# Normalisation transposes in a PSUM bank of their own behind the state update, and the GLU second in the tail

## The chip, the cores and the metric

The kernel runs on one core of a Trainium2 chip. The metric is the time on the device of one execution, in microseconds (us), the median of several runs. The engines are named as in the profile: PE is TensorE (matmuls; PEld its weight loads), DVE is VectorE, ACT is ScalarE, POOL is GpSimd, SP is SyncE, which here only issues DMAs.

## The reference

One layer of a streaming encoder: a prompt of 1024 rows and 8 samples of 16 rows, together T = 1152 rows of width 1024. One input projection feeds four mixers: "a" (S5 state space with GELU and a GLU), "b" (sparse attention), "c" (gated delta rule) and "d" (gated linear attention, GLA). Then

```
x <- LayerNorm(alpha * x + W_out( sum_b sigmoid(r_b(x)) * P_b( silu(z_b(x)) * M_b(x) ) ))
```

For the change, the end of one block of "c" and "d" matters. With state s (per head, 128x128 in "c", 64x128 in "d"):

```
# c, per block
v_new = u_blk - w_blk s
o = exp(gc) * (q s) + ((q k^T) * decay) v_new
s = exp(g_last) * s + (k * exp(g_last - gc))^T v_new
# d, per block
o = A v + (q * exp(bc)) s
s = exp(b_last) * s + (k * exp(b_last - bc))^T v
# both, after all blocks
o = o * rsqrt(mean(o*o) + 1e-6) * norm          # then gated with silu(z)
```

and for "a", `g = y @ w_glu; y = g[:512] * sigmoid(g[512:])`.

## The kernel before

Everything is fp32; large products are made of three fp32r matmuls (`mm3`, L189 to L191: high by high, low by high, high by low), with the operands split into a high part by ACT and a low part by DVE or POOL.

Tiles of 128 rows: nine of them, 0 to 7 the prompt, 8 the samples. The program is written stage after stage, and a planner that simulates the engines lays down, ahead of time, the order of instructions on every engine. It prefers what has the higher priority among what it believes ready: DMA loads and splits marked urgent first, then the mixers and the tail in the order of the program, then, as filler, the products of the input projection (`gemm_t`, tile pg). On the chip each engine works its list in order, and a semaphore wait holds up all behind it.

PSUM has eight banks: two for pg, two for pn, four for pm. `pmt` hands out the four pm banks in turn, in the order of the program; nearly all products and transposes of sparse attention, delta rule and linear attention go through them, and so do the final products (L1834 region, tile fin).

Delta rule, `gdn_tile(i)`, for each tile i: loads; small products that finish a triangular inverse (m1, u1, x1); then products kq, pv, kn, ks (L978), qs (L983), each evacuated by DVE (L960, L965, L970, L980, L984); vn (L1009), copied to VN by ACT; oi (L1014), from which DVE makes o (L1020). Then `rms_gate`: ACT squares o, DVE makes rsqrt of the mean in small steps (L652 to L657), scales o (L1063), PE transposes it into the pm tile py (L1066), DVE multiplies with norm and gate (L1068) and SP stores to `YD["c"]`. After it the state update: S products (L1025) from kdec and VN, and DVE adds them to the state (L1030). Tile 8 updates eight sample states, four heads one after another, loading and storing them (L1041 to L1051). Most tiles of this stage have one buffer. The state K.S of tile i is read by ks and qs of tile i+1.

Linear attention has the same shape: `gla_levels` for two tiles (seven levels, products lv, L1209), then `gla_scan` for each: glo (L1278), `rms_gate` into `YD["d"]`, then the state products glS (L1289) and updates (L1295). Tile 8 comes first here. `s5` ("a") runs beside delta rule; it uses pn and DVE.

The tail. `mix_branch` reads a branch's output from `YD` in three chunks of 384 rows, splits it, and for 8 column tiles x 3 chunks makes 12 matmuls each into a PSUM tile (mix); DVE multiplies with the merge gate (L1785) and adds to ACC (L1786, from the second branch on). `s5_glu` reads S5's output (12 loads), makes 8 x 3 tiles (glu); the even column tiles go through Tanh on ACT (L1731), the odd ones through DVE twice (L1735, L1737) and are stored to `YD["a"]` (L1738), which `mix_branch` of "a" loads again (L1756). There are four Y buffers: the three chunks of the present step and the first of the next. The order is "b", "c", GLU, "a", "d", then `finish` with W_out and LayerNorm. Tail products that are ready fill PE while linear attention still runs.

Of the kernel before, what the change touches and what calls it, by code (L numbers as in the profile page):

```python
# [67 lines left out]
def setup(K):  # L68
    nc, tc, ctx = K.nc, K.tc, K.ctx
    K.prio, K.kind = {"hi": 0, "lo": 20000000}, None  # L70
    tc.cur_priority = 10000000
    K.const = ctx.enter_context(tc.tile_pool(name="const", bufs=1))
    K.dram = ctx.enter_context(tc.tile_pool(name="dram", bufs=1, space=DRAM))
    K.pg = ctx.enter_context(tc.tile_pool(name="pg", bufs=2, space=PSUM))
    K.pm = ctx.enter_context(tc.tile_pool(name="pm", bufs=4, space=PSUM))
    K.pn = ctx.enter_context(tc.tile_pool(name="pn", bufs=2, space=PSUM))
    c = K.const
    ii = c.tile([128, 128], I32, name="ii")
    K.ident = c.tile([128, 128], F32, name="ident")
    with urgent(K):  # L80
        nc.gpsimd.iota(ii, pattern=[[1, 128]], base=0, channel_multiplier=-1)
        nc.vector.tensor_scalar(K.ident, ii, 0.0, None, op0=OP.is_equal)
    K.colmrow = ii
    K.bd = c.tile([128, 128], F32, name="bd")
    with tc.tile_pool(name="bdp", bufs=1) as t:
        r16 = t.tile([128, 128], I32, name="r16")
        nc.gpsimd.iota(r16, pattern=[[16, 8], [0, 16]], base=0, channel_multiplier=-1)
        hi = t.tile([128, 128], F32, name="hi16")
        nc.vector.tensor_scalar(hi, r16, 0.0, None, op0=OP.is_le)
        lo = t.tile([128, 128], F32, name="lo16")  # L90
        nc.vector.tensor_scalar(lo, r16, -15.0, None, op0=OP.is_ge)
        nc.vector.tensor_tensor(K.bd, hi, lo, op=OP.mult)
    K.bdneg = c.tile([128, 128], F32, name="bdneg")
    nc.vector.tensor_scalar(K.bdneg, K.bd, BIG, -BIG, op0=OP.mult, op1=OP.add)
# [797 lines left out]
def gdn_tile(K, i, tp):  # L892
# [125 lines left out]
    else:  # L1018
        for h in range(4):
            nc.vector.scalar_tensor_tensor(o[:, h], po[:, H4[h]], rq[:, h:h + 1], tmp[:, h], op0=OP.mult, op1=OP.add)  # L1020
    rms_gate(K, o, K.gnorm, gt, tp, "c", s)
    if i < 8:
        pS = pmt(K, "S")
        for h in range(4):
            nc.tensor.matmul(pS[:, H4[h]], kdec[:, h], VN[:, h], start=True, stop=True)  # L1025
        if i == 0:
            nc.vector.tensor_copy(K.S, v4(pS))
        else:
            for h in range(4):
                nc.vector.scalar_tensor_tensor(K.S[:, h], K.S[:, h], eg[:, h:h + 1], pS[:, H4[h]], op0=OP.mult, op1=OP.add)  # L1030
        if i == 7:
            nc.sync.dma_start(O["p_gdn"].rearrange("h k v -> k h v"), K.S)
    else:
        ge = tp.tile([128, 4, 8], F32, tag="ge", name="ge")
        gb = tp.tile([128, 4, 8], F32, tag="gb", name="gb")
        nc.vector.tensor_tensor(gb, K.g[:, 8, :, None].to_broadcast([128, 4, 8]), K.bm[:, None, :].to_broadcast([128, 4, 8]), op=OP.mult)
        pg = pmt(K, "ge")
        nc.tensor.matmul(pg[:, 0:32], K.ones, gb.rearrange("p h b -> p (h b)"), start=True, stop=True)
        nc.scalar.activation(ge.rearrange("p h b -> p (h b)"), pg[:, 0:32], AF.Exp)
        for h in range(4):  # L1040
            S8 = tp.tile([128, 8, 128], F32, tag="S8", name="S8")  # L1041
            nc.sync.dma_start(S8, s8(I["state_gdn"], h))
            for q in range(2):
                vm = tp.tile([128, 4, 128], F32, tag="vt", name="vm")
                nc.vector.tensor_tensor(vm, VN[:, h, None, :].to_broadcast([128, 4, 128]), bc(K.bm[:, q * 4:q * 4 + 4]), op=OP.mult)
                pS = pmt(K, "S8")
                nc.tensor.matmul(pS, kdec[:, h], vm.rearrange("p b v -> p (b v)"), start=True, stop=True)
                for b in range(4):
                    bb = q * 4 + b
                    nc.vector.scalar_tensor_tensor(S8[:, bb], S8[:, bb], ge[:, h, bb:bb + 1], pS[:, H4[b]], op0=OP.mult, op1=OP.add)  # L1050
            nc.sync.dma_start(s8(O["s_gdn"], h), S8)  # L1051


def rms_gate(K, o, norm, gt, tp, br, s):

    nc = K.nc
    ss = tp.tile([128, 4], F32, tag="oss", name="oss")
    junk = tp.tile([128, 128], F32, tag="ojunk", name="ojunk")
    for h in range(4):
        nc.scalar.activation(junk, o[:, h], AF.Square, accum_out=ss[:, h:h + 1])  # L1060
    nc.vector.tensor_scalar(ss, ss, 1.0 / 128.0, 1e-6, op0=OP.mult, op1=OP.add)
    rsqrt(K, ss, ss, tp, 4)
    nc.vector.tensor_tensor(o, o, bc(ss), op=OP.mult)  # L1063
    py = pmt(K, "py")
    for h in range(4):
        nc.tensor.transpose(py[:, h * 128:(h + 1) * 128], o[:, h], K.ident)  # L1066
    yt = tp.tile([128, 4, 128], F32, tag="oyt", name="oyt")
    nc.vector.scalar_tensor_tensor(yt, py.rearrange("p (h t) -> p h t", h=4), norm, gt, op0=OP.mult, op1=OP.mult)  # L1068
    nc.sync.dma_start(K.YD[br].rearrange("(j p) t -> p j t", p=128)[:, :, s], yt)
# [148 lines left out]
def gla_scan(K, i, AT, tp):  # L1218
# [63 lines left out]
        nc.vector.tensor_copy(o, pov)  # L1282
    else:
        nc.vector.tensor_tensor(o, pov, oi, op=OP.add)
    rms_gate(K, o, K.dnorm, gt, tp, "d", s)
    if i < 8:
        for j in range(2):
            pS = pmt(K, "glS")
# [11 lines left out]
    else:  # L1300
# [19 lines left out]
        for z in range(2):  # L1320
            for h in range(4):
                nc.gpsimd.dma_start(O["s_gla"][z::2, h].rearrange("b k v -> k b v"), S8[z * 64:z * 64 + 64, h])


def gla(K):
# [463 lines left out]
def tail(K):  # L1789
    tc = K.tc  # L1790
    with tc.tile_pool(name="mx", bufs=2) as p, tc.tile_pool(name="ap", bufs=1) as ap, \
            tc.tile_pool(name="yb", bufs=3) as yp:
        K.ACC = ap.tile([128, 8, T], F32R, name="ACC")
        K.wo = K.ctx.enter_context(tc.tile_pool(name="wo", bufs=1, side="right"))
        mix_branch(K, 0, "b", yp, p)
        mix_branch(K, 1, "c", yp, p)
        s5_glu(K, 2, yp, p)
        mix_branch(K, 3, "a", yp, p)
        mix_branch(K, 4, "d", yp, p, last=True)
        finish(K, yp, p)  # L1800
# [159 lines left out]
def build(ctx, tc, I, O, stages, dev=None):  # L1960
# [15 lines left out]
    with tc.tile_pool(name="xp", bufs=1) as K.xp, ExitStack() as wn, ExitStack() as nat:  # L1976
# [3 lines left out]
        with tc.tile_pool(name="cvc", bufs=1) as K.cvc:  # L1980
            gdn_prepare(K)
            K.glmask = gla_masks(K)
            with tc.tile_pool(name="bp", bufs=1) as K.bp:
                with ExitStack() as cv:
                    natural_cols(K)
                    nat.close()
                    project_q(K)

                    def between():
                        project_rest(K, "end" in stages)  # L1990
                        wn.close()
                        K.cvp = cv.enter_context(tc.tile_pool(name="cvp", bufs=2, side="right"))
                        project(K, "end" in stages)
                    dsa(K, between)
            if "c" in stages:
                gdn(K)
            gdn_conv_state(K)
# [38 lines left out]
```

## Time and profile before

| | us |
|---|---|
| median of 3 runs | 1908.05 (1903.02 to 1910.44) |
| the profiled execution | 1909.76 |
| its span, first to last instruction | 1908.0 |
| PE busy | 1804.6 |
| DVE busy | 1447.6 |
| ACT busy | 670.9 |
| POOL busy | 270.9 |

The mean granted clock of PE was 0.982 of full speed. The clock has two levels, 1.2 and 2.4 GHz, which the views show as 0.50 and 1.00; a stretch between them had both. In a timeline, the number in brackets is how long the engine sat idle before the instruction, and what released it. A matmul's duration overlaps with that of the next, so counts in a stretch say more than durations.

### The profile page before, as it was taken

To read this page: it belongs to the slowest core of one execution; us is meant where nothing else is said; L and a number is where in the kernel's file an instruction comes from. 1 tells how busy PE (TensorE), PEld (TensorE's weight loads), DVE (VectorE), ACT (ScalarE), POOL (GpSimd) and SP (SyncE) were. 2 spreads that over 40 slices of the span, in tenths; PEclk is the share of its full clock that TensorE was granted. 3 is DMA by queue.
4 is the path that set the end of the run, shared out by engine and by line. 5 is a ranking of instruction groups with operands and counts; after the bars stand their busy time and mean duration, and the time that the engine had idled before them with its cause. 6 is when DMAs were issued, how large, how long until landed. Compare 5 with 4: busy or idle time off the path is not lost.

```text
span 1908.0 us, 31158 instructions
## 1 busy us (share of the span) xinstructions
PE 1804.6 (95%) x10962; PEld 1710.1 (90%) x10962; DVE 1447.6 (76%) x3914; ACT 670.9 (35%) x1535; POOL 270.9 (14%) x297
## 2 busy tenths in 40 slices
PE   8999999999999999998989989899898999979997
PEld 7989999999989999997889888888888998979986
DVE  6289999944999997368890279976657899857776
ACT  4261211233666656245321333332373233222200
POOL 1110222111222210101211112211232000000000
PEclk9999999999999999999999899999999999989999
DMA  6322322232323212467335545444455673376422
GB/s 192 99 67 74 89 90 84 90 101 86 96 75 84 69 55 67 115 214 232 102 96 136 160 134 144 139 134 128 123 166 166 188 173 104 109 229 188 143 88 89
DMA packets 345290, 234.54 MB, mean 123 GB/s; under 512 B 82891, under 2 KB 327419, under 8 KB 345134
## 3 DMA queue, kind: packets, MB, share of 16 engines
q1 hardware_dynamic: 337262, 220.88, 40.1%
q10 hardware_dynamic: 7488, 10.62, 1.5%
q8 instruction: 87, 1.43, 0.3%
q0 software_dynamic: 384, 1.05, 0.2%
q14 instruction: 69, 0.57, 0.1%
HBM read 156.12 MB, written 76.35 MB: 122 GB/s over the span
## 4 chain that ended last, share of the span: by engine, by line
PE 39%; DVE 13%; DMA 5%; issue 3%; ACT 2%; POOL 1%; SPq 1%; DVEq 0%; POOLq 0%; ACTq 0%
PE pg L190 4%; PE pg L191 4%; PE pg L189 4%; PE mix L189 3%; PE mix L190 3%; PE mix L191 3%; PE fin L191 2%; PE fin L190 2%; PE fin L189 2%; PE lv L1209 1%; PE glu L191 1%; PE glu L190 1%; PE glu L189 1%; DMA S<-in_state_gdn 1%; DVE pb L870 1%
## 5 line engine op out<-in xcount | busy, mean ns | idle before, releaser
L189 PE MATMUL pg<-XH,whi 128*128 128x384 f32 x1648 | 564.0, 342 | 0.9 <-DVE gth L238 0.9
L190 PE MATMUL pg<-XL,whi 128*128 128x384 f32 x1648 | 564.3, 342 | 0.0
L191 PE MATMUL pg<-XH,wlo 128*128 128x384 f32 x1648 | 563.4, 342 | 0.0
L189 PEld LDWEIGHTS pg<-XH,whi 128*128 128x128 f32 x1648 | 312.7, 190 | 5.2 <-issue 1.8
L191 PEld LDWEIGHTS pg<-XH,wlo 128*128 128x128 f32 x1648 | 312.5, 190 | 4.1 <-issue 2.0
L190 PEld LDWEIGHTS pg<-XL,whi 128*128 128x128 f32 x1648 | 312.6, 190 | 3.1 <-issue 1.1
L109 ACT CAST whi<-wst 128x1024 fp32r<-128x1024 f32 (+2 forms) x121 | 109.5, 907 | 253.6 <-PE pg L190 118.1
L110 POOL TENSOR_TENSOR wlo<-wst,whi 128x1024 fp32r<-128x1024 f32 x44 | 109.6, 2492 | 335.3 <-ACT whi L109 329.6
L189 PE MATMUL mix<-YH,whi 128*128 128x384 f32 x384 | 132.7, 347 | 13.1 <-ACT YH L112 9.4
L110 DVE TENSOR_TENSOR wlo<-wst,whi 128x512 fp32r<-128x512 f32 (+2 forms) x77 | 76.4, 993 | 77.5 <-ACT whi L109 76.6
L190 PE MATMUL mix<-YL,whi 128*128 128x384 f32 x384 | 131.9, 344 | 1.1 <-DVE YL L113 1.1
L191 PE MATMUL mix<-YH,wlo 128*128 128x384 f32 x384 | 131.9, 344 | 0.0
L1684 ACT ACTIVATE mth<-pg 128x384 f32<-128x384 f32 x96 | 46.7, 487 | 138.3 <-PE pg L191 95.6
L392 DVE TENSOR_SCALAR_CACHE_REDUCE tkj<-mk,tk_c 128x384 bf16<-128x384 f32 (+6 forms) x112 | 90.9, 875 | 0.6
L392 DVE TENSOR_SCALAR_CACHE_REDUCE tkj<-tkh,tk_c 128x384 bf16<-128x384 bf16 (+6 forms) x112 | 90.9, 876 | 0.5
L189 PEld LDWEIGHTS mix<-YH,whi 128*128 128x128 f32 x384 | 73.4, 192 | 15.2 <-ACT YH L112 10.0
L190 PEld LDWEIGHTS mix<-YL,whi 128*128 128x128 f32 x384 | 73.3, 191 | 1.6 <-DVE YL L113 1.5
L191 PEld LDWEIGHTS mix<-YH,wlo 128*128 128x128 f32 x384 | 73.3, 191 | 0.0
L715 DVE SCALAR_TENSOR_TENSOR cy<-rb,cw,cy 128x384 f32<-128x384 f32 (+1 forms) x108 | 71.2, 659 | 2.8 <-ACT cy L713 2.2
L535 ACT ACTIVATE pr<-pr,sm 128x256 f32<-128x256 f32 (+7 forms) x72 | 53.7, 747 | 13.7 <-DVE sm L534 13.5
L1785 DVE SCALAR_TENSOR_TENSOR mth<-mth,mix 128x384 f32<-128x384 f32 x72 | 39.0, 549 | 24.1 <-PE mix L191 12.0
L502 POOL TENSOR_TENSOR mb<-BT,mk 128x512 f32<-128x512 f32 (+1 forms) x32 | 42.8, 1340 | 97.9 <-DVE mx L529 94.7
(630 smaller groups left out, 3794.9 us busy)
## 6 DMA issues: line engine op xcount, KB each, us to landing
wst<-in_w_in SPq DMA_DIRECT2D x80, 512.0 KB
wst<-in_w_branch SPq DMA_DIRECT2D x32, 256.0 KB
gk<-cq SPq DMA_DIRECT2D x27, 256.0 KB
merge_b<-mth SPq DMA_DIRECT2D x24, 192.0 KB
cq<-cy SPq DMA_DIRECT2D x24, 192.0 KB
merge_c<-mth SPq DMA_DIRECT2D x24, 192.0 KB
kq<-cq SPq DMA_DIRECT2D x18, 256.0 KB
merge_d<-mth SPq DMA_DIRECT2D x24, 192.0 KB
```

The source lines that it names most:

```text
L109: nc.scalar.copy(hi, src)
L110: (eng or nc.vector).tensor_tensor(lo, src, hi.bitcast(F32), op=OP.subtract)
L189: nc.tensor.matmul(ps, lh, rh, start=start, stop=False)
L190: nc.tensor.matmul(ps, lh, rl, start=False, stop=False)
L191: return nc.tensor.matmul(ps, ll, rh, start=False, stop=stop)
L392: nc.vector.tensor_scalar(junk[a % 2][:, :ns[a]], up[a] if bit > 15 else sc[a], cand[:, a:a + 1].bitcast(F32), None, op0=OP.is_ge, op1=OP.add,
L502: bias = nc.gpsimd.tensor_tensor(mbv, bt[:, 2 * jj:2 * jj + 2, ::-1][:, :, 256 - band:], mk[:, None, off:n].to_broadcast([128, 2, band]), ...
L535: nc.scalar.activation(p[:, r, 0:n], p[:, r, 0:n], AF.Exp, bias=sm[:, 2 + r:3 + r], scale=1.0, accum_out=sm[:, r:r + 1])
L715: nc.vector.scalar_tensor_tensor(yc, rb[:, i:i + c], K.cw[:, i * 12 + a:i * 12 + a + 1], yc, op0=OP.mult, op1=OP.add)
L870: nc.vector.tensor_tensor(pb[:, lo:bs, 0:lo], ab[:, j, lo:bs, None].to_broadcast([n, bs - lo, lo]), xb[:, j, None, 0:lo].to_broadcast([n, ...
L1684: nc.scalar.activation(th[:, :n], ps, AF.Tanh, scale=0.5)
L1785: nc.vector.scalar_tensor_tensor(th, th, 1.0, ps, op0=OP.add, op1=OP.mult)
```

## The change

The pool pm is made last of the three PSUM pools and closed after sparse attention; a pool of three banks takes its place (same tag, handed out by `pmt`), and the freed bank becomes a pool pr, for py alone. In `gdn_tile` and `gla_scan` the call of `rms_gate` moves behind the state update. In the tail, `s5_glu` changes places with branch "c"; the first argument only says which Y buffers are used.

```diff
@@ setup
     K.pg = ctx.enter_context(tc.tile_pool(name="pg", bufs=2, space=PSUM))
-    K.pm = ctx.enter_context(tc.tile_pool(name="pm", bufs=4, space=PSUM))
     K.pn = ctx.enter_context(tc.tile_pool(name="pn", bufs=2, space=PSUM))
+    K.pm4 = ExitStack()
+    K.pm = K.pm4.enter_context(tc.tile_pool(name="pm", bufs=4, space=PSUM))
@@ gdn_tile
-    rms_gate(K, o, K.gnorm, gt, tp, "c", s)
     if i < 8:
         pS = pmt(K, "S")
...
             nc.sync.dma_start(s8(O["s_gdn"], h), S8)
+    rms_gate(K, o, K.gnorm, gt, tp, "c", s)
@@ rms_gate
-    py = pmt(K, "py")
+    py = K.pr.tile([128, 512], F32, tag="py", name="py")
@@ gla_scan
-    rms_gate(K, o, K.dnorm, gt, tp, "d", s)
     if i < 8:
         for j in range(2):
             pS = pmt(K, "glS")
...
                 nc.gpsimd.dma_start(O["s_gla"][z::2, h].rearrange("b k v -> k b v"), S8[z * 64:z * 64 + 64, h])
+    rms_gate(K, o, K.dnorm, gt, tp, "d", s)
@@ tail
         mix_branch(K, 0, "b", yp, p)
-        mix_branch(K, 1, "c", yp, p)
-        s5_glu(K, 2, yp, p)
+        s5_glu(K, 1, yp, p)
+        mix_branch(K, 2, "c", yp, p)
         mix_branch(K, 3, "a", yp, p)
         mix_branch(K, 4, "d", yp, p, last=True)
@@ build
                     dsa(K, between)
+            K.pm4.close()
+            K.pm = ctx.enter_context(tc.tile_pool(name="pm3", bufs=3, space=PSUM))
+            K.pr = ctx.enter_context(tc.tile_pool(name="pr", bufs=1, space=PSUM))
             if "c" in stages:
                 gdn(K)
```

## Rows read from the trace of the kernel before

**Rows 1.** The page, busy time of each engine, share of the span, instructions.

```profile
PE 1804.6 (95%) x10962; PEld 1710.1 (90%) x10962; DVE 1447.6 (76%) x3914; ACT 670.9 (35%) x1535; POOL 270.9 (14%) x297
```

**Rows 2.** Busy time by stage: PE, PEld, DVE, ACT, POOL; PE clock, DMA share, GB/s.

```profile
1050.00:1280.00 230.00, 207.19 (x1491) 189.76 (x1489) 176.20 (x509) 79.66 (x236) 49.12 (x41) 0.96 0.49 141
1280.00:1420.00 140.00, 130.97 (x765) 121.30 (x765) 85.20 (x196) 57.89 (x99) 31.06 (x35) 0.98 0.47 137
1420.00:1655.00 235.00, 221.98 (x1375) 213.66 (x1374) 206.06 (x487) 75.25 (x178) 17.16 (x17) 0.99 0.54 150
1685.00:1701.00 16.00, 6.35 (x21) 5.95 (x22) 6.53 (x7) 3.39 (x3) 0.00 (x0) 0.68 0.68 217
1701.00:1800.00 99.00, 98.26 (x557) 97.56 (x556) 72.69 (x118) 24.68 (x28) 0.00 (x0) 1.00 0.65 204
```

**Rows 3.** What PE waited for: us in total, times, longest.

```profile
PE mix L189 <- ACT YH L112: 9.4, 2, 8.6
PE py L1066 <- DVE o L1063: 8.7, 5, 4.2
...
PE cs L734 <- DVE S L1050: 4.8, 2, 3.1
...
PE mix L189 <- DVE mth L1785: 3.2, 3, 2.2
...
PE qs L983 <- DVE P L960: 2.2, 2, 1.1
```

**Rows 4.** Timeline, the end of the GLU and the start of branch "a".

```profile
1684.30 0.32 SPq L1738 DMA_DIRECT2D y_a<-glgt  x1
...
1687.52 1.33 SPq L1756 DMA_DIRECT2D yl<-y_a  x2
...
1692.01 1.48 ACT L112 ACTIVATE YH<-yl 128x1536 fp32r<-128x1536 f32 x1 [6.58 <-DMA yl<-y_a]
...
1693.54 0.69 PE L189 MATMUL mix<-YH,whi 128*128 128x384 f32 x1 [8.64 <-ACT YH L112]
...
1696.66 0.32 SPq L1738 DMA_DIRECT2D y_a<-glgt  x1
```

**Rows 5.** Busy time in three stretches of 2 us, columns as in rows 2.

```profile
1230.00:1232.00 2.00, 1.49 (x11) 1.23 (x11) 2.00 (x5) 0.00 (x0) 0.00 (x0) 1.00 0.26 73
1274.00:1276.00 2.00, 2.00 (x10) 2.00 (x11) 1.97 (x4) 0.00 (x0) 0.99 (x1) 0.50 0.06 18
1698.00:1700.00 2.00, 2.00 (x8) 2.00 (x8) 1.00 (x3) 0.00 (x0) 0.00 (x0) 0.50 0.54 118
```

**Rows 6.** Instructions grouped by line, DVE in the tail.

```profile
L1786 DVE TENSOR_TENSOR ACC<-ACC,mth 128x384 f32<-128x384 f32 x72 | 39.2, 553 | 0.8
L1785 DVE SCALAR_TENSOR_TENSOR mth<-mth,mix 128x384 f32<-128x384 f32 x72 | 39.0, 549 | 24.1 <-PE mix L191 12.0 <-DMA mth<-merge_d 5.1 <-DMA mth<-merge_a 2.9
...
L1737 DVE SCALAR_TENSOR_TENSOR glgt<-glth,glgt 128x384 f32<-128x384 f32 x12 | 10.2, 856 | 0.8 <-DMA glgt<-gate_a 0.5
...
L1735 DVE SCALAR_TENSOR_TENSOR glth<-glth,glu 128x384 f32<-128x384 f32 x12 | 6.5, 551 | 4.1 <-PE glu L191 4.1
```

**Rows 7.** Timeline of PE, the end of delta-rule tile 7.

```profile
1258.77 1.05 PE L1014 MATMUL oi<-VN,P 128*128 128x128 f32 x8
...
1273.92 1.11 PE L1066 MATMUL py<-ident,o 128*128 128x128 f32 x4 [4.16 <-DVE o L1063]
1274.83 1.91 PE L1025 MATMUL S<-VN,kdec 128*128 128x128 f32 x8
```

**Rows 8.** All S products: count, duration, first and last start.

```profile
L1025 PE MATMUL S<-VN,kdec x64: 275/275/418, 1081.8 to 1276.3; 128*128 128x128 f32 x64
```

**Rows 9.** Timeline of DVE, the same tile.

```profile
1260.38 1.12 DVE L1020 SCALAR_TENSOR_TENSOR o<-oi,rq,tmp 128x128 f32<-128x128 f32 x4
...
1273.19 0.67 DVE L1063 TENSOR_TENSOR o<-o,oss 128x512 f32<-128x512 f32 x1
```

**Rows 10.** Timeline of PE, delta-rule tile 6.

```profile
1230.51 1.16 PE L983 MATMUL qs<-S,kq 128*128 128x128 f32 x8 [1.12 <-DVE P L960]
```

## The prediction

> **What bounds the kernel now.** I read the page's busy table first, then busy time by stage, then what TensorE (PE) waited for, and last the timeline at two places. PE is busy 1804.6 us of 1908.0 [rows 1]. No later engine can hide that: the work of PE is the same after the change, so the time can fall only where PE stands idle or runs at its lower clock. The stages [rows 2] say where that is. From 1050 to 1420 us (delta rule, with S5 beside it and w_in products as filler) PE is idle 230 - 207.2 + 140 - 131.0 = 31.8 us. From 1420 to 1655 us (linear attention, with filler and the first tail products) it is idle 235 - 222.0 = 13.0 us. From 1685 to 1701 us it does 21 matmuls in 16 us, at a mean clock of 0.68. After that it is full: 557 matmuls in 99 us, 98.26 us busy, which is 0.176 us a matmul.
>
> So a chain that gets shorter on VectorE (DVE) or ScalarE (ACT) is worth nothing in itself. It counts only by the PE stalls that go with it. The list of PE's waits [rows 3] names those: 9.4 us before a mix product for YH, 8.7 us in five waits of the normalisation transposes py, 4.8 us at the conv-state transposes, 3.2 us of mix products for a PSUM bank that L1785 frees, 2.2 us at L983 for a bank that L960 frees. Because the engine works its queue in order, each is a hole in everything, filler too.
>
> **GLU second.** The 9.4 us is the step from the GLU to branch "a". The timeline there [rows 4] shows the chain: a GLU store to y_a is issued at 1684.30, the reload yl<-y_a at 1687.52, ACT starts the split at 1692.01, PE starts at 1693.54 after 8.64 us idle. The twelfth GLU store is issued only at 1696.66, so the third chunk comes later still. PE then runs at granted clock 0.50, the 1.2 GHz level, from 1698 to 1700 [rows 5], after having stood still; 8 matmuls take those 2 us, against 11.4 at 0.176 us. The whole price of the step: 16 us in which 21 x 0.176 = 3.7 us of work was done [rows 2], so 12.3 us. With the change branch "c" (8 x 3 x 12 = 288 matmuls, about 51 us at 0.176) lies between the GLU's last store and branch "a", and the chain of some 10 us is hidden by it five times over. What is late next: at the new steps GLU to "c" and "c" to "a" the operand is ready in DRAM long before, as it is now at "a" to "d", and that step lies inside the stretch 1701 to 1800 where PE lost 0.7 us in all. If the cover were gone, the 12.3 us would be back. I take a gain of 12, with bounds 10 and 13.
>
> The GLU's own loads move too: twelve y loads, the weight and gate loads and twelve stores on SP's queue, 50 to 75 us earlier, past the loads of "c" and among those of linear attention. What can be hurt is linear attention's own loads, where one stands behind them in the queue. I take 0, with a bound of 2.2 us on the bad side (the 2.2 us hole of L983 as the nearest row for a short queue upset).
>
> On DVE a branch tile costs 0.549 + 0.553 us (L1785, L1786), a GLU tile half as often 0.551 + 0.856 us (L1735, L1737), so 0.70 us on the mean [rows 6]. In the stretch where linear attention keeps DVE busy 206 of 235 us [rows 2], 24 GLU tiles stand in place of 24 tiles of "c": 24 x 0.4 = 9.6 us less DVE work there. PE waits 3.2 us for L1785 in the whole run [rows 3]. I take 1 of these, bounds 0 and 3.2.
>
> **State update ahead of the normalisation.** No instruction is added or taken away: nine tiles each of delta rule and linear attention, four transposes, the same DVE and ACT operations, the same store. What changes is the order and the bank. The S products need only VN and kdec. Yet in delta-rule tile 7 they start at 1274.83, 16.1 us after the oi products at 1258.77 and directly behind py at 1273.92 [rows 7]: py sits ahead of S in one ring of four banks and must wait for the chain on DVE, L1020 at 1260.38 to L1063 at 1273.19 [rows 9], lengthened by S5 operations queued between. The eight S groups lie from 1081.8 to 1276.3 [rows 8], so a tile takes about (1274.8 - 1081.8) / 7 = 27.6 us, of which S waits 16 in tile 7. After the change S can follow oi at once and the next tile's first products need no longer stand behind py. My estimate is that a tile falls to between 14 and 20 us and that delta rule ends 60 to 100 us earlier. That moves no end by itself: the filler now used there is used later, PE's work is the same.
>
> What counts is py's holes: 8.7 us [rows 3], and after the longest (4.16 us) PE ran at 0.50 from 1274 to 1276 [rows 5, 7]. That is 2 us at half rate, 1 us lost, so py's price is some 9.7 us. The transposes still wait for the same DVE chain, and they still stand in PE's queue at a place fixed ahead of time. Only the work that was stuck behind them (S, the next tile's products) now has a chance to come before. I take 4 of 9.7, bounds 0 and 9.7. The normalisation now starts behind the four S updates on DVE, and in the last tile behind the whole update of the sample states; the only reader of its store is a tail branch, so this is 0. The next tile's gate load (L908) waits on SP for L1068, now later, and weight loads stand behind it: two weight buffers of 72 matmuls each (12.7 us at 0.176) cover a few us, 0 again. The conv-state transposes (4.8 us) wait for the last state updates, which the change brings ahead of the normalisation but does not shorten: 0.
>
> By the Trainium skill, "TensorE: Matmul & The Clock Gate", section "HAM oscillation", PSUM double-buffering on top of a loop already kept dense gave no further gain (126.6 against 125.5 us). By that rule a private bank would be worth 0 and the sum would end 4 us later; the row of py differs in kind, as the bank here holds back other work, and no run here shows it yet.
>
> **Three banks for the rest.** From delta rule on, every other pm tile turns through three banks. Now PE already waits at L983, the fifth product group of a tile, for the bank that the first group's evacuation frees: 1.12 us at 1230.51 [rows 10], 2.2 us in two of eight tiles [rows 3]. With three banks L978 waits for L960 and L983 for L965. Where the order puts filler in between, nothing is lost; where DVE is late it costs about 1.1 us. Bounds: 0, and two waits in each of nine tiles, 18 x 1.1 = 20 us. The waits happen now in a quarter of the tiles, so I take 2 of them more, about 2 us. In linear attention one bank per level is in use and DVE sets the pace: 0. The final products use one bank in 24 matmuls (5 us), evacuated in well under that: 0. Closing the old pool and opening the new one falls between sparse attention and delta rule, where filler is at hand: 0.
>
> **Sum.** 12 + 1 + 4 - 2 = 15 us less. The profiled execution took 1909.76 us (span 1908.0 and 1.76 us around it), 1.7 us above the median 1908.05. 1909.76 - 15 = 1894.8; on the scale of the median 1893.
>
> **The rivals.** (a) The forecast, 1888 to 1898 us, chance 0.45.
>
> (b) The shorter recurrence also takes a good part of the other holes of delta rule with it: 31.8 us of idle from 1050 to 1420 us, of which py explains 8.7 us. For it: the same S5 and delta-rule work met DVE at 176 of 230 us, so DVE has room. Against it: most of the holes are S5's, and each belongs to one operation that still waits for one DVE result. If half of the 31.8 goes, the gain is 12 + 1 + 16 = 29 us: 1909.76 - 29 - 1.7 = 1879. Chance 0.2.
>
> (c) The gain of the GLU step is given back: the new order of the queues after 850 us opens holes elsewhere, or linear attention, ended early, no longer covers the step from the w_in filler to the first mix products. The nearest price is the GLU hole itself with its slow restart, 12.3 us; a half of it, 6 us, and no gain from py leaves 12 + 1 - 2 - 6 = 5: 1903. Chance 0.22.
>
> (d) Three banks become the bound: two bank waits in every delta-rule tile, 20 us, and the lower clock after them. It takes the place of py's wait, at L978 and L983. A restart at 1.2 GHz cost 1 us after a hole of 4 us [rows 5]; five such are 5 us. 20 + 5 - 13 = 12 us slower: 1909.76 + 12 - 1.7 = 1920. It decides for "slower" from 22.5 us on (13 of gain and 9.5 of bound), that is 1.25 us in each of the 18 waits. For it: L983 waits already with four banks. Against it: filler is always at hand in that stage. The Trainium skill names the effect, same page, section "A second HAM failure mode: psum-queue depth-cycling": PE that pauses shortly between groups as it cycles through banks falls back in clock. In the trace the clock stays at 1.00 through the 1.12 us pause at L983 [rows 5]. Chance 0.08.
>
> (e) The change does nothing, because the transposes and the GLU step keep the holes they have: 1908. Against it stands the 51 us of cover. Chance 0.05.
>
> **Range and chances.** A measurement of this kernel tells from no change about 0.5%, 9.5 us; faster is below 1898.5, slower above 1917.6. Faster: (b), 0.43 of (a) and 0.03 of (c), 0.66. Same: 0.02 of (a), 0.17 of (c) and (e), 0.24. Slower: (d) and 0.02 of (c), where the holes are deeper than any now, 0.10. The range runs from 1873, (b) with 22 of the 31.8 us instead of 16, to 1907, the far side of (c); outside lie (d), (e) and the edges of (b) and (c), about 0.2. The likeliest case alone has 1888 to 1898.
>
> **What would show it.** The window of the GLU's end has no hole: PE busy over 9.5 us in each 10 us from the first tail products to the final ones, the wait "mix for ACT YH" falls from 9.4 us to under 2, and the clock stays 1.00 there. In a delta-rule tile the S products start within 3 us of the oi products, py comes after them, and the period of S falls from 27.6 us to under 20. The waits of py fall to 2 to 6 us, those at L978 and L983 rise from 2.2 to 3 to 6 us. The last S group starts before 1230 us, and the w_in filler ends later than now. The prediction is wrong if the idle time of PE between 850 and 1420 us grows by more than 10 us, if waits at L978 and L983 exceed 15 us, or if linear attention ends before the filler and leaves PE without work at the step into the tail.

## The result and the profile after

The changed kernel takes 1931.55 us (median of 4 runs, 1929.77 to 1935.93) against 1905.53 us for the kernel before in the same comparison: ratio 1.0137, 95% interval 1.0106 to 1.0168. It is 26 us slower. The forecast was 1893 us, faster; the range ended at 1907. The profiled execution has a span of 1934.1 us. Lines of the program after the setup are numbered one higher than before, but for those of the state updates (L1025, L1289, L1295), which keep their numbers.

The page's busy line (columns as in [rows 1]):

```profile
PE 1816.4 (94%) x10962; PEld 1722.1 (89%) x10962; DVE 1441.3 (75%) x3914; ACT 671.3 (35%) x1535; POOL 271.0 (14%) x297
```

No instruction came or went. PE is busy 12 us longer for the same 10,962 matmuls, so part of the loss is a lower clock (0.974 of full speed on the mean; before, 0.982). The same stages as in [rows 2], same columns:

```profile
1050.00:1280.00 230.00, 210.26 (x1513) 189.97 (x1512) 173.03 (x541) 79.48 (x242) 43.68 (x37) 0.96 0.56 159
1280.00:1420.00 140.00, 123.80 (x713) 118.50 (x712) 81.81 (x160) 57.48 (x89) 33.82 (x38) 0.95 0.36 102
1420.00:1655.00 235.00, 204.32 (x1213) 193.75 (x1212) 187.49 (x473) 73.00 (x185) 19.76 (x19) 0.92 0.49 138
1685.00:1701.00 16.00, 14.84 (x85) 14.51 (x84) 11.26 (x21) 1.86 (x3) 0.00 (x0) 1.00 0.61 191
```

Read the matmul counts against [rows 2]. The hole at the GLU's end is gone (85 matmuls in 16 us in place of 21). The first stage does 22 more, the second 52 fewer. The third, 1420 to 1655 us, does 162 fewer: at 0.176 us each that is 28.5 us, the size of the whole loss; the 30 fewer of the first two stages and the 64 more at the GLU's end stand beside it. In the third stage PE idles 30.7 us instead of 13.0, and the clock falls from 0.99 to 0.92.

What PE waited for, columns as in [rows 3]:

```profile
PE s5y L1618 <- DVE HS L1596: 14.0, 4, 5.1
PE lv L1210 <- DVE X L1205: 13.5, 7, 3.3
...
PE lv L1210 <- DVE rs_t L657: 6.9, 3, 2.7
...
PE s5y L1618 <- DVE HF L1597: 4.2, 1, 4.2
...
PE mix L190 <- ACT YH L113: 3.3, 1, 3.3
...
PE py L1067 <- DVE glo L1064: 0.6, 2, 0.3
...
PE ks L979 <- DVE P L961: 0.2, 1, 0.2
```

Of the waits that the prediction spoke of, py in the delta rule fell from 8.7 us to nothing, the conv-state transposes from 4.8 to nothing and the bank waits at ks and qs from 2.2 to 0.2. YH fell from 9.4 to 3.3 us; these stand at 1500.0 us, at the start of branch "b", and none is left at branch "a". Two others grew, at s5y (S5) and at lv (linear attention), whose own code the change doesn't touch. In the kernel before they were

```profile
PE lv L1209 <- DVE X L1204: 8.1, 7, 2.3
...
PE s5y L1617 <- DVE HS L1595: 4.4, 2, 2.4
```

so s5y waits 9.6 us longer for HS, and lv 5.4 longer for X and 6.9 for rs_t, a step of `rms_gate`.

In the delta rule the state update does what was forecast. All S products (as [rows 8]), the transposes of linear attention and its level products, in the view of one tile (count, duration ns, first and last start):

```profile
L1025 PE MATMUL S<-VN,kdec x64: 274/275/276, 1066.7 to 1194.9; 128*128 128x128 f32 x64
...
L1067 PE MATMUL py<-ident,glo x36: 271/273/473, 1469.7 to 1615.1; 128*128 128x128 f32 x36
...
L1210 PE MATMUL lv<-glZ,X x240: 270/275/552, 1430.4 to 1598.8; 128*128 128x128 f32 x120
```

A tile takes (1194.1 - 1066.7) / 7 = 18.2 us instead of 27.6. But linear attention starts no earlier (1430.4; before, 1423.2): S5 lies ahead of it and ends at 1420. And it is now done at 1615.1, where it took until 1674.3. It runs in 185 us instead of 251, and this is where the work is missing. A timeline of PE shows how (duration, then in brackets the idle time before and its releaser):

```profile
1537.50 0.34 PE L192 MATMUL mix<-YH,wlo 128*128 128x384 f32 x1
1540.52 1.13 PE L1210 MATMUL lv<-glZ,X 128*128 128x128 f32 x8 [2.68 <-DVE rs_t L657]
1541.99 1.11 PE L1067 MATMUL py<-ident,glo 128*128 128x128 f32 x4 [0.34 <-DVE glo L1064]
1545.32 2.05 PE L1210 MATMUL lv<-glZ,X 128*128 128x128 f32 x8 [2.21 <-DVE rs_t L657]
1547.15 1.06 PE L1067 MATMUL py<-ident,glo 128*128 128x128 f32 x4
1550.11 1.13 PE L1210 MATMUL lv<-glZ,X 128*128 128x128 f32 x8 [1.89 <-DVE X L1205]
1553.32 2.05 PE L1210 MATMUL lv<-glZ,X 128*128 128x128 f32 x8 [2.08 <-DVE X L1205]
1555.02 0.67 PE L190 MATMUL mix<-YH,whi 128*128 128x384 f32 x1
```

From 1537.8 to 1555.0 there is no filler: PE steps from one small product of linear attention to the next. At 1555.0 the mix products of branch "b" resume. The DVE timeline says why there and not earlier. L1784 is what empties a mix tile of "b" from its PSUM bank:

```profile
1516.95 1.01 DVE L1784 SCALAR_TENSOR_TENSOR ACC<-mth,mix 128x384 f32<-128x384 f32 x2
...
1521.08 0.55 DVE L1784 SCALAR_TENSOR_TENSOR ACC<-mth,mix 128x384 f32<-128x384 f32 x1
...
1532.33 0.56 DVE L1784 SCALAR_TENSOR_TENSOR ACC<-mth,mix 128x384 f32<-128x384 f32 x1
...
1554.09 0.55 DVE L1784 SCALAR_TENSOR_TENSOR ACC<-mth,mix 128x384 f32<-128x384 f32 x1
...
1557.90 1.01 DVE L1784 SCALAR_TENSOR_TENSOR ACC<-mth,mix 128x384 f32<-128x384 f32 x2
```

Counted off at 12 matmuls a tile, tiles 5 to 8 of "b" end on PE at 1521.9, 1524.9, 1533.8 and 1537.8; they are emptied at 1554.1, 1557.9, 1558.4 and 1562.9, so 32, 33, 25 and 25 us later. Mix tiles have four banks, two of pg and two of pn. With four unemptied tiles no ninth can start, and it starts 0.4 us after tile 5 is out. In the kernel before, tile 1 waited 32 us as well (here 49), but tiles 2 to 8 were emptied 1.7 to 6.3 us after their last matmul. A late operand is not the reason for tile 5: its merge gate is the second of the three loads that SP issues from 1518.86 us on, 34 us before:

```profile
1518.86 3.12 SPq L1781 DMA_DIRECT2D mth<-merge_b  x3
```

Two narrow windows show both phases (columns as in [rows 2]):

```profile
1516.00:1538.00 22.00, 21.34 (x124) 20.10 (x124) 19.64 (x53) 8.39 (x29) 1.31 (x1) 0.88 0.66 165
1538.00:1555.00 17.00, 7.96 (x40) 6.89 (x41) 15.59 (x46) 2.52 (x4) 0.00 (x0) 0.71 0.23 62
```

In the second, DVE is busy 15.6 of 17 us with linear attention's own chain, PE 8.0 of 17 at a clock of 0.71.

### The profile page after: what moved, and what is told of

The parts are those of the page before. It is cut to its first block, busy times and chain, and to the rows that moved or that the text cites. A ratio compares the mean times of both kernels' runs of the same rounds, so it can differ in the third digit from the quotient of the medians.

```text
span 1934.1 us, 31202 instructions
## 1 busy us (share of the span) xinstructions
PE 1816.4 (94%) x10962; PEld 1722.1 (89%) x10962; DVE 1441.3 (75%) x3914; ACT 671.3 (35%) x1535; POOL 271.0 (14%) x297
## 4 chain that ended last, share of the span: by engine, by line
PE 40%; DVE 14%; DMA 7%; issue 2%; ACT 2%; SPq 1%; POOL 1%; DVEq 0%; POOLq 0%; ACTq 0%
PE pg L192 5%; PE pg L191 5%; PE pg L190 5%; PE mix L190 3%; PE mix L191 2%; PE mix L192 2%; PE fin L191 2%; PE fin L190 2%; PE fin L192 2%; PE lv L1210 1%; DMA wos<-in_w_out 1%; PE glu L192 1%; PE glu L190 1%; PE glu L191 1%; DMA gk<-cq 1%
## 5 line engine op out<-in xcount | busy, mean ns | idle before, releaser
L111 POOL TENSOR_TENSOR wlo<-wst,whi 128x1024 fp32r<-128x1024 f32 x44 | 110.9, 2522 | 378.2 <-ACT whi L110 357.1
L111 DVE TENSOR_TENSOR wlo<-wst,whi 128x512 fp32r<-128x512 f32 (+2 forms) x77 | 76.5, 995 | 82.5 <-ACT whi L110 82.1
L1210 PE MATMUL lv<-glZ,X 128*128 128x128 f32 x240 | 39.3, 312 | 25.3 <-DVE X L1205 13.5
L1210 PEld LDWEIGHTS lv<-glZ,X 128*128 128x128 f32 x240 | 34.9, 219 | 30.3 <-issue 24.3
```

The lines of the kernel that those rows point to most:

```text
L111: (eng or nc.vector).tensor_tensor(lo, src, hi.bitcast(F32), op=OP.subtract)
L1210: nc.tensor.matmul(ps[:, o:o + 128], x[:, j, z * 128:z * 128 + 128], Z[:, j, :, z * 64:z * 64 + 64], start=True, stop=True)
```

## The experiments

To compare stages that end at different times, "lost" below is PE's idle time plus its busy time multiplied by (1 - granted clock), summed over windows of 2 us. The stages end with the last sample-state product of the delta rule, the last transpose of S5 (hf), the last py of linear attention, and the first final product (fin). One execution each; kernels that share a stage's code differ there by some 5 us. A stage is not equally long in all kernels: where the delta rule ends earlier, the stretch of S5 after it is longer by about as much.

| kernel | 820 to 1050 | delta rule | S5 after it | linear attention | to fin | fin at |
|---|---|---|---|---|---|---|
| before | 24.5 | 35.1 | 9.1 | 15.7 | 13.2 | 1800 |
| changed | 28.1 | 22.3 | 26.7 | 43.8 | 1.2 | 1826 |
| glu_only | 22.0 | 29.8 | 7.9 | 16.6 | 0.0 | 1779 |
| order_glu | 23.0 | 30.6 | 10.8 | 21.7 | 0.0 | 1786 |
| bank_in_d | 22.6 | 30.4 | 6.6 | 42.9 | 1.5 | 1809 |
| bank_in_c | 25.8 | 20.3 | 28.6 | 21.9 | 1.1 | 1802 |
| bank_c_evac | 28.1 | 23.0 | 30.6 | 19.0 | 0.0 | 1802 |
| s5_first | 26.2 | 28.9 | 30.0 | 23.3 | 0.1 | 1810 |
| evac_first | 26.3 | 20.4 | 26.9 | 26.2 | 2.7 | 1807 |
| gla_old_order | 23.8 | 20.8 | 26.6 | 44.7 | 3.4 | 1821 |
| glu_third | 26.6 | 24.3 | 26.6 | 39.4 | 22.8 | 1843 |
| three_banks | 28.3 | 45.5 | 4.1 | 20.6 | 12.3 | 1813 |
| bank_only | 26.8 | 26.4 | 32.9 | 48.6 | 21.9 | 1860 |
| glu_evac_first | 21.8 | 27.2 | 7.6 | 18.2 | 0.0 | 1777 |

Four theories stood at the start. **1:** the new order inside linear attention leaves PE without work. **2:** the GLU in second place does. **3:** three banks are too few. **4:** py's own bank uncouples linear attention: more of its DVE work is ready early, goes ahead of the tail's evacuations, the four mix banks stay full, and PE runs out of filler.

**The GLU alone (glu_only).** The kernel before with only the tail's order changed.

```diff
-        mix_branch(K, 1, "c", yp, p)
-        s5_glu(K, 2, yp, p)
+        s5_glu(K, 1, yp, p)
+        mix_branch(K, 2, "c", yp, p)
```

> The kernel before with only the GLU second in the tail. Theory 1 (the reordered linear attention starves PE of filler): the hole behind the GLU, 12.3 us, goes and nothing else changes: 1891 to 1896 us against 1905 of before. Theory 2 (the GLU as second step starves PE while linear attention runs): 1915 to 1930, with PE holes between 1420 and 1680 us. Theory 3 (three banks): as theory 1.

Measured: 1893.64 us against 1906.95, ratio 0.993 (0.9908 to 0.9952). Theory 2 falls. Linear attention's window is as before the change ([rows 2]), and the GLU's end has no hole; first and second line:

```profile
1420.00:1655.00 235.00, 223.15 (x1382) 214.76 (x1381) 204.65 (x484) 75.97 (x176) 13.41 (x15) 0.99 0.56 159
1670.00:1686.00 16.00, 16.00 (x93) 16.00 (x92) 12.71 (x19) 6.34 (x6) 0.00 (x0) 1.00 0.90 281
```

**The changed kernel with linear attention's old order (gla_old_order).**

```diff
@@ gla_scan
+    rms_gate(K, o, K.dnorm, gt, tp, "d", s)
     if i < 8:
...
-    rms_gate(K, o, K.dnorm, gt, tp, "d", s)
```

> The changed kernel with the normalisation of linear attention alone put back ahead of its state update (py still in its own bank). Theory 1: PE idle in the linear-attention stage falls from 30 to about 12 us and the time to 1900 to 1910. Theory 2 and theory 3: no change, 1925 to 1935.

Measured: 1933.12 us, ratio 1.0149 (1.0125 to 1.0174): the changed kernel's time, 44.7 us lost in linear attention. Theory 1 falls.

**The changed kernel with the old order of the tail (glu_third).**

```diff
-        s5_glu(K, 1, yp, p)
-        mix_branch(K, 2, "c", yp, p)
+        mix_branch(K, 1, "c", yp, p)
+        s5_glu(K, 2, yp, p)
```

> The changed kernel with the old order of the tail (b, c, GLU, a, d). Theory 2: the filler is back, 1905 to 1915. Theory 1 and theory 3: nothing is won in linear attention and the hole behind the GLU returns: 1938 to 1945, or the same 1931 if the GLU now ends well ahead of linear attention.

Measured: 1952.45 us, ratio 1.0244 (1.0221 to 1.0267), above every forecast and 21 us slower than the changed kernel. GLU second helps there too.

**The banks alone (bank_only).** Three banks and py's own bank; both old orders, GLU third.

```diff
+            K.pm = ctx.enter_context(tc.tile_pool(name="pm3", bufs=3, space=PSUM))
+            K.pr = ctx.enter_context(tc.tile_pool(name="pr", bufs=1, space=PSUM))
...
-    py = pmt(K, "py")
+    py = K.pr.tile([128, 512], F32, tag="py", name="py")
```

> The kernel before with only the banks changed: three for pm from delta rule on and one for py, normalisation and tail in the old order. Theory 3 (three banks hold PE up): 1920 to 1930, with waits at the ks, qs and lv products of over 10 us more. Theories 1 and 2: 1900 to 1910.

Measured: 1961.34 us, ratio 1.0289 (1.0251 to 1.0327), slower than any theory had it. The banks alone carry the loss; with both new orders beside them (glu_third) the time is 9 us shorter. Whether it is the missing fourth bank or py's own one, this run can't say: the next parts them.

**Three banks without the fourth (three_banks).** As bank_only, but py stays in the ring and the eighth bank lies unused; against bank_only:

```diff
-            K.pr = ctx.enter_context(tc.tile_pool(name="pr", bufs=1, space=PSUM))
...
-    py = K.pr.tile([128, 512], F32, tag="py", name="py")
+    py = pmt(K, "py")
```

> The kernel before with three banks for pm from delta rule on, py among them as before, the fourth bank unused. Theory 4 (py's own bank lets linear attention run on without a pause, its DVE instructions are listed ahead of the evacuations of the tail products, which then fill their four banks and stop PE): linear attention is held up by py as before, 1900 to 1915 us, evacuations 0 to 6 us after the products. Theory 3 (three banks are too few): 1940 to 1965, as with the banks changed alone.

Measured: 1915.34 us, ratio 1.0048 (1.003 to 1.0066). The pair differs by py's bank alone, and the kernel that has a bank less is 46 us faster. The window of linear attention, three_banks:

```profile
1420.00:1655.00 235.00, 217.88 (x1334) 209.25 (x1334) 198.89 (x476) 77.22 (x172) 20.39 (x22) 0.98 0.53 148
```

and bank_only:

```profile
1420.00:1655.00 235.00, 196.96 (x1141) 187.07 (x1140) 186.19 (x478) 78.39 (x188) 23.51 (x28) 0.88 0.47 130
```

Counted off as above, tiles 2 to 12 of "b" are emptied 0 to 6.3 us after their last matmul in three_banks; in bank_only tiles 2 to 4 wait 27 to 34 us, and tiles 8 to 11 wait 18 to 20. The late evacuations come with py's bank. Too few banks cost some 9 us (three_banks against its kernel before), so theory 3 explains a third of the 26 us at most. The S products tell the same of the delta rule (three_banks first):

```profile
L1026 PE MATMUL S<-VN,kdec x64: 274/276/422, 1081.9 to 1287.2; 128*128 128x128 f32 x64
```

```profile
L1026 PE MATMUL S<-VN,kdec x64: 275/275/275, 1067.1 to 1194.6; 128*128 128x128 f32 x64
```

With the old order but its own bank (bank_only) the period is 18.1 us, with the ring of three 29 us. The bank is what frees the recurrence; what the order does without it, order_glu shows below.

**Evacuations first (evac_first, glu_evac_first).** The changed kernel; the tail's DVE evacuations get the planner's highest priority, that of loads and splits.

```diff
@@ s5_glu, mix_branch
-            nc.vector.scalar_tensor_tensor(th[t], th[t], 1.0, ps, op0=OP.add, op1=OP.mult)
+            with urgent(K):
+                nc.vector.scalar_tensor_tensor(th[t], th[t], 1.0, ps, op0=OP.add, op1=OP.mult)
...
+            with urgent(K):
                 if n == 0:
...
```

> The changed kernel with the DVE instructions that free the tail's PSUM banks (L1784 to L1787 and the first of the odd GLU tiles) at the urgent priority, ahead of linear attention's. Theory 4: evacuations come within 6 us of their products instead of 15 to 33, PE idle from 1490 to 1620 us falls from 25 to under 12 us, and the time to 1895 to 1910. Theory 3: products still wait elsewhere, 1925 to 1935.

The same two edits on glu_only, as the control:

> The kernel before with the GLU second and the same urgent evacuations. Theory 4: evacuations were not late there, so little changes: 1885 to 1897, at most the 3 us of waits for L1785. Theory 3: the same.

Measured: 1920.0 us, ratio 1.0074 (1.0047 to 1.0101), against the changed kernel's 1.0137; linear attention loses 26.2 instead of 43.8 us. The time lies between the forecasts of theory 4 (1895 to 1910 us) and theory 3 (1925 to 1935). The control is at 1893.61 us, ratio 0.9927 (0.9903 to 0.9952), the same as glu_only. So late evacuations cost the changed kernel 12 to 18 us and glu_only nothing. Against its control evac_first loses 8.0 us more in linear attention and 19.3 more beside S5: most of what it still lacks is in another stage. From tile 9 of "b" on the evacuations come at once. Tiles 4 to 7 still wait 13 to 17 us (8 to 12 in the control): the merge gates of tiles 4 to 6, whose products end by 1510.3 us, are loaded only from 1516.05 us on. evac_first's SP and DVE timelines:

```profile
1516.05 1.70 SPq L1782 DMA_DIRECT2D mth<-merge_b  x3
...
1522.11 1.47 DVE L1786 SCALAR_TENSOR_TENSOR ACC<-mth,mix 128x384 f32<-128x384 f32 x3
...
1537.55 0.55 DVE L1786 SCALAR_TENSOR_TENSOR ACC<-mth,mix 128x384 f32<-128x384 f32 x1 [0.68 <-PE mix L192]
...
1540.67 0.55 DVE L1786 SCALAR_TENSOR_TENSOR ACC<-mth,mix 128x384 f32<-128x384 f32 x1
```

**Own bank and new order in the delta rule alone (bank_in_c).** Four banks and the old order from S5 on, GLU second.

```diff
+    py = K.pr.tile([128, 512], F32, tag="py", name="py") if br == "c" else pmt(K, "py")
...
             gdn_conv_state(K)
+            pm3.close()
+            K.pm = ctx.enter_context(tc.tile_pool(name="pm5", bufs=4, space=PSUM))
```

> The changed kernel with py's own bank and the later normalisation in delta rule alone; after it pm has four banks again, and linear attention is as in the kernel before; GLU second. Theory 4: linear attention takes its old 220 us and the tail products fill it: 1888 to 1900. If the loss came from delta rule and S5: 1915 to 1930. Theory 3: as theory 4, unless three banks hurt in delta rule.

Measured: 1913.33 us, ratio 1.0047 (1.0022 to 1.0072), between the two forecasts and nearer to the second. Linear attention is nearly back (21.9 lost), yet the kernel is 20 us behind glu_only: the delta rule saves 9.5 us of PE time and the stretch of S5 after it loses 20.7 more. That places 11 of the 20 us; 3.8 more are lost before 1050 us and 5.3 more in linear attention, each no larger than the difference between kernels of the same code. Its waits from 1270 to 1420 us:

```profile
PE s5y L1618 <- DVE HS L1596: 11.9, 3, 5.1
PE s5y L1618 <- DVE HF L1597: 4.2, 1, 4.2
```

**Own bank and new order in linear attention alone (bank_in_d).** The pools change places after S5; delta rule and S5 as before, GLU second.

```diff
+    py = K.pr.tile([128, 512], F32, tag="py", name="py") if br == "d" else pmt(K, "py")
...
                 s5(K)
+            K.pm4.close()
+            K.pm = ctx.enter_context(tc.tile_pool(name="pm3", bufs=3, space=PSUM))
+            K.pr = ctx.enter_context(tc.tile_pool(name="pr", bufs=1, space=PSUM))
```

> GLU second; the delta rule and S5 as in the kernel before with four banks, and py's own bank, the three banks and the new order only from linear attention on. Theory 4 gives the linear attention's part of the loss alone: its TensorE loss rises from 16.6 to 40 us or more, the S5 stage stays at 8 us, the time is 1915 to 1922 us. Its rival, that linear attention loses because it inherits what a faster delta rule left undone on VectorE at the end of S5, gives 1893 to 1898 us with a loss under 22 us.

Measured: 1921.8 us, ratio 1.0068 (1.0044 to 1.0092), 28 us above glu_only, with 42.9 us lost in linear attention and 6.6 beside S5. Theory 4's place is confirmed, and the loss is not inherited from the faster delta rule. Counted off as above, tiles 2 to 5 of "b" are emptied 21 to 25 us after their last matmul, and tiles 9 to 12 after 16 to 22 us; in glu_only it is 2.7 to 9.5 us, and nothing.

```profile
1420.00:1655.00 235.00, 206.37 (x1224) 196.97 (x1223) 191.77 (x480) 73.68 (x185) 13.59 (x15) 0.92 0.49 137
```

**Both new orders without the bank (order_glu).** GLU second, `rms_gate` behind the state update twice, py in the ring of four; against glu_only:

```diff
@@ gdn_tile (and the same in gla_scan, with K.dnorm and "d")
-    rms_gate(K, o, K.gnorm, gt, tp, "c", s)
     if i < 8:
...
+    rms_gate(K, o, K.gnorm, gt, tp, "c", s)
```

> GLU second and both rms_gate calls behind the state update, but py stays in the ring of four banks, with no bank of its own. Theory 4 (py's own bank lets linear attention's VectorE work run ahead of the tail's evacuations) gives 1893 us, within 4 us of GLU second alone, with linear attention's TensorE loss at 16 to 18 us as in GLU second alone (16.6), since the ring still ties py to the other tiles. Had the order been what does it, the loss would be near the changed kernel's 43.8 us and the time 1910 to 1920 us. Had the order alone carried the delta rule's saving, the time would be 1880 to 1888 us.

Measured: 1896.01 us, ratio 0.9941 (0.9916 to 0.9965), glu_only within the error. The order alone is worth nothing; linear attention loses 21.7 us, where 16 to 18 were forecast, a difference of the size of the noise between executions. The order does put the S products 0.9 to 1.0 us behind oi in every tile, but the period stays at 25.8 us (27.3 in glu_only).

**What S5 loses (bank_c_evac, s5_first).** bank_in_c with the urgent evacuations of evac_first, and bank_in_c with S5's scan chain urgent:

```diff
@@ s5_part
-    cross(W, SX[:, :, 0:128])
+    with urgent(K):
+        cross(W, SX[:, :, 0:128])
...
+        nc.vector.tensor_copy(K.HF[:, 0, gs], W[:, :, 127])
```

> Own bank and new order in the delta rule alone (four banks and old order from S5 on), GLU second, and the tail's VectorE evacuations in the urgent group. Without urgent evacuations this was 1913.3 us with 28.6 us lost beside S5 and 21.9 in linear attention. Theory 4: what is lost beside S5 waits for S5's own chain, not for an evacuation, so urgent evacuations leave 27 to 29 us there; linear attention falls to 17 to 20; the time is 1908 to 1913 us, still 15 us above GLU second alone. Its rival, that late evacuations also make the loss beside S5, gives 1893 to 1898 us.

> Own bank and new order in the delta rule alone, GLU second (1913.3 us, 28.6 us of TensorE lost beside S5 after the delta rule's end), and S5's scan chain on VectorE, from the first rotation to the two HS and HF copies, in the urgent group. The theory is that the faster delta rule pushes S5's rounds back on VectorE, so that three rounds instead of two are left for the stretch where S5 is alone and their serial chain makes TensorE wait at s5y. It expects two rounds or fewer after 1300 us, the s5y waits of 16 us down by half or more, a loss beside S5 of 10 to 20 us and a time of 1900 to 1906 us. Its rival, that S5's rounds are serial whatever VectorE does first and their pace is set elsewhere (TensorE's fixed order, the wlo splits on GpSimd beside the scan), leaves three rounds there, 27 to 30 us lost and 1911 to 1916 us.

Measured: bank_c_evac 1908.64 us, ratio 0.9995 (0.9978 to 1.0013), 30.6 us lost beside S5; s5_first 1915.98 us, ratio 1.005 (1.0027 to 1.0073), 30.0 lost. Urgent evacuations gain 5 us over bank_in_c (10 by the ratios), but none of it beside S5. My theory of S5 fell: its last three rounds still lie after 1300 us, and the waits from 1270 to 1426 us are no smaller:

```profile
PE s5y L1619 <- DVE HS L1597: 15.4, 3, 5.4
```

The urgent chain is only a part of a round. In the fourth round the way from SX to the copy of HS fell from 20.0 us (bank_in_c) to 11.7, but the way from the third copy of HS to that SX, which the edit leaves alone, rose from 40.9 to 63.6 us. No run moved that part.

## Why the prediction was wrong, step by step

**GLU second: right.** 12 + 1 us forecast, 13.3 measured (1906.95 - 1893.64). The cover of 51 us of branch "c" held.

**State update ahead: mechanism right in part.** S follows oi within 0.9 us, the period fell to 18.2 us (14 to 20 forecast), the holes of py vanished: 8.7 us, of which I had taken 4, and with them the 4.8 us of the conv-state transposes, put at 0. The delta rule's stretch lost 13 us less than before (7.5 less than in glu_only, whose delta rule is the old one). But I put it down to the order; bank_only has the old order and a period of 18.1 us, and order_glu has the new one, a period of 25.8 us, and gains nothing. The timeline of the changed delta rule:

```profile
1175.43 1.05 PE L1015 MATMUL oi<-VN,P 128*128 128x128 f32 x8
1176.32 1.06 PE L1025 MATMUL S<-VN,kdec 128*128 128x128 f32 x8
...
1188.49 1.05 PE L979 MATMUL ks<-S,kq 128*128 128x128 f32 x8
...
1191.24 0.60 PE L1067 MATMUL py<-ident,o 128*128 128x128 f32 x4
```

py of one tile now comes 15 us after S (9 to 17 in the other tiles), behind the next tile's first products, and PE no longer waits for it.

**The first failed step: "That moves no end by itself: the filler now used there is used later".** It is not neutral. S5 ends when it did (1420 us against 1413), so a delta rule that ends 77 us earlier (1265 us against 1342) only lengthens the stretch in which S5 and filler are alone. There PE stops at s5y for S5's scan; 204 matmuls of the filler (pg) were still to come after 1420 us, so filler existed, but not at that place of PE's list. At the longest of these waits the product listed behind it is the next one of a filler tile already begun, with weights that were in use before the wait:

```profile
1347.94 0.34 PE L190 MATMUL pg<-XH,whi 128*128 128x384 f32 x1
1353.38 1.30 PE L1618 MATMUL s5y<-HS,OM 128*128 128x144 f32 x4 [5.09 <-DVE HS L1596]
1354.30 0.69 PE L191 MATMUL pg<-XL,whi 128*128 128x384 f32 x1
```

In the delta rule alone (bank_in_c) this costs 20 us net where I had +4 - 2; 11 of them stand in the delta rule and beside S5. S5 falls behind while the delta rule runs its fast tiles: its third and fourth copies of HS come at 1142 and 1204 us, at 1127 and 1169 in the kernel before. Why its rounds don't move up instead is open: neither evacuations (bank_c_evac) nor DVE's priority for the scan (s5_first) is the cause; the steps of a round before the scan were left untested. What the runs show is place and size.

**The second: "In linear attention one bank per level is in use and DVE sets the pace: 0".** This is the larger one: 28 us (bank_in_d against glu_only). I priced the bank as something that can only be missing. In the ring of four, py's place in turn held linear attention back, and that left DVE time for the tail's evacuations. With a bank of its own py no longer holds it back. The program order puts linear attention's DVE work ahead of the tail's, so the evacuations come 25 to 33 us late, four banks fill, and PE, which does its list in order, is left with a chain whose every link waits for DVE. Evacuations first gives back 12 us of the time and 17.6 of the 28.1 us lost more in this stretch; the rest was not taken apart (the late merge gates in evac_first may be a part of it). That the ring held linear attention back, and that the evacuations come late without it, is shown by the pair three_banks and bank_only; that the planner's order on DVE is the reason is argued from the timelines and from evac_first.

The two parts don't add fully: 20 and 28 us over glu_only alone, 38 together (1931.55 - 1893.64). These are differences of medians from different comparisons; by the ratios they are 22, 26 and 39 us.

**Three banks, rival (d).** The ring of three costs some 9 us (three_banks), half of my bad bound, but not at its place: the changed kernel waits 0.2 us at ks and none at qs, and three_banks 0.8 us at ks; its waits are py's, 10.9 us. Rival (c) named the right family (holes opened elsewhere), with a price of 6 to 12 us; the place and the size were not in it. My sign of failure, idle time from 850 to 1420 us up by more than 10 us, did not show the loss: it rose only from 50.5 to 55.0 us.

By the Trainium skill, "TensorE: Matmul & The Clock Gate", section "HAM oscillation", PSUM double-buffering on top of a loop made dense gave no further gain (126.6 against 125.5 us). The runs here differ from it in both directions: py's own bank (bank_only against three_banks) lowered the loss of the delta rule from 45.5 to 26.4 us and raised the losses of linear attention from 20.6 to 48.6 and of S5 after the delta rule from 4.1 to 32.9. In this kernel a bank also decides what may run ahead. The same page's section "A second HAM failure mode: psum-queue depth-cycling" says that short pauses between groups, in a kernel that cycles through PSUM banks, bring the clock down; the trace agrees where filler is missing: four pauses of 1.9 to 2.7 us between groups from 1538 to 1555 us, clock 0.71.

The best version among these runs is glu_only, ratio 0.993: the GLU second and nothing else.

## What to carry to other kernels

A ring of buffers is also a throttle: before a tile is taken out of it, ask which work it was holding back, on which engine that work will now run ahead, and whose evacuations stand behind it there. Where PE lives on filler, a shorter chain isn't free: see where the next serial stage begins and ends, and whether the filler's own banks are emptied by the engine that the chain keeps busy. For each part of a change run that part alone; here one part gave 13 us, hidden under two that took 38 together.

## What the runs showed of the hardware

Part of S5's late scan is DVE standing still behind POOL. In the changed kernel L1593 takes 679 to 692 ns as a rule, but 1035, 2800 and 2830 in three of eight rounds; L1607 of 32 elements takes 0.19 us, and once 2.22. Each of these four times POOL splits a weight tile (L111) beside it. Timeline of DVE and POOL, two of them:

```profile
1348.11 2.35 POOL L111 TENSOR_TENSOR wlo<-wst,whi 128x1024 fp32r<-128x1024 f32 x1 [0.75 <-ACT whi L110]
1348.18 2.83 DVE L1593 TENSOR_TENSOR W<-W,CO 128x512 f32<-128x512 f32 x1
...
1387.23 2.67 POOL L111 TENSOR_TENSOR wlo<-wst,whi 128x1024 fp32r<-128x1024 f32 x1
1387.73 2.22 DVE L1607 TENSOR_TENSOR f<-f,t 128x32 f32<-128x32 f32 x1
```

L1593 ends 0.55 us after POOL (1351.01 against 1350.46), as it does the two other times; L1607 ends within 0.1 us of it (1389.95 against 1389.90): DVE waited here until POOL's instruction was over. The Trainium skill says so on "SBUF — State Buffer", section "SBUF: two separate sides": a port pair that DVE, with two SBUF inputs, and GpSimd take in turns, for a whole instruction. The trace agrees. Two microseconds of the 12 us from SX to HS, in two of S5's last three rounds, are this wait; no run here moved the splits, so what they cost the kernel is not shown. The kernel before has such waits too: there L1603 takes 2.28 us at 1360.8 us in place of 0.19, beside such a split.
